# Joint 512-column products in four output projections and in the products for the memory's keys

## The chip, the cores and the metric

The kernel runs on one core of one Trainium2 chip. The metric is the device time of one execution in microseconds (us). Three runs of the kernel before gave 1250.81, 1250.83 and 1251.04 us; their median is 1250.83 us.

## The reference

Two transformer blocks follow each other on an activation of 256 tokens by 1024 features, all in float32. The first has a gated feed-forward, a mixer (latent attention with 8 heads beside differential attention with 4), an output projection, a second feed-forward and a gated embedding. The second has two layers of mixer, cross attention to a memory of 256 tokens, and feed-forward, each closed by a residual and a layer norm. Cut to what the change touches:

```python
h = h + jnp.concatenate([o_mla, o_diff], axis=-1) @ w_out[i]            # block one
h = h + 0.5 * swiglu(rms_norm(h, g_ffn2[i]), ...)
...
y = hybrid_ab_mixer(...)                 # layer 0; ends with y @ w_out; layer 1: a pooling mixer
x = layer_norm(ALPHA * x + y, ln_mix_g[l], ln_mix_b[l])
k = (mem_n @ w_k).reshape(B, -1, XA_HEADS, XA_DH)                       # keys of the memory
...
x = layer_norm(ALPHA * x + o @ w_o, ln_xa_g[l], ln_xa_b[l])
y = swiglu_ffn(x, ffn_wg[l], ffn_wu[l], ffn_wd[l])
```

## The kernel before

**Tiles and split operands.** Activations lie transposed, eight blocks of 128 features by 256 tokens. A float32 product is made of three products in the fp32r type: each weight is split into a rounded part `hi` and the rest `lo`, each activation into 256 columns of its rounded part and, beside them in the same tile, 256 columns of its rest. A weight tile of 128 by 128 then needs hi by rounded, hi by rest and lo by rounded. All three go into one PSUM accumulator of 256 columns, so that a tile takes three matmuls of 256 columns.

**The joint form**, which the kernel already has in the feed-forward products (argument `joint` of `gen_T`, line 364), lets hi pass over all 512 columns in one matmul and fills a whole PSUM bank of 512 columns. Rounded and rest come out in two halves of the bank, and they are added when the bank is read: `summed` (line 430) copies the right half to SBUF on ScalarE and adds the left half on VectorE.

```python
s = self.St(name)
self.ac.copy(s, o[:, T:])
self.ve.tensor_tensor(s, s, o[:, :T], ALU.add)
```

**Order of the work.** No scheduler reorders anything: each engine runs its instructions in the order in which the program issues them (`manual_schedule`, line 2172). A unit is eight weight tiles (1024 columns). `Net.get` (line 232), called before the products of unit u, issues the ScalarE cast that makes `hi` of unit u + 4 and the VectorE subtraction that makes `lo` of unit u + 3 (lines 319 and 343), then a step of the work put off by `later`. The weights come by DMA on the SP queue into three raw buffers.

**The output projections.** `row_tiles(NB, NB, head)` (line 739) orders the 64 tiles: the first `head` output blocks j run side by side over all eight k, so that they end together, one tile after the other; then each further block takes one unit of its own. The head is 4 for `wout` of block one (lines 902 to 910, read out by `evac_out`), 3 for `abo` of the hybrid mixer (line 1931) and 4 for `xo0` and `xo1` of the cross attentions (line 1873). Each of them reads a finished accumulator with one VectorE instruction that also adds the residual (line 904, or line 1918 in `residual`). What follows is `enter` (line 785) or `Norm.add` (line 678). Both issue, per block, on ScalarE the scaled rounded copy (line 791 or 687) and the square (line 535); on VectorE, put off by one block, the rest of the split (line 795 or 691) and the running sums (lines 547 and 550), one sum for `enter` and two for `Norm.add`.

```python
ac.activation(xs[:, :T], z, AF.Copy, scale=g)
sq = self.stats.square(z)

def rest():
    ve.scalar_tensor_tensor(xs[:, W:W + T], z, g, xs[:, :T].bitcast(F32), ALU.mult, ALU.subtract)
    self.stats.accumulate(z, sq)
```

Once the eighth block is in, `Rows` (line 623) makes the statistics between the first units of the next product: `columns` transposes the running sums on TensorE into `tot` (line 564), VectorE reduces them (line 566), GpSimd takes the reciprocal root (lines 612 and 613), and two units later TensorE broadcasts the result into `pb` (line 512). The next product needs the split blocks `xs` as its moving operand, and its own read-outs need `pb`.

**The memory's keys.** `mem_kv` (line 1488) makes eight blocks of keys for each of the two layers, one unit of products each, in a three-matmul loop of its own, read out by one ScalarE copy (line 1504). The 16 units are fillers: the program drops them (`filler.fill`) between steps of the mixers where TensorE would otherwise wait. Seven of them stand in the mixer of block one: two among its first products, three between the steps of the differential attention (`diff_s` with line 1008, `diff_c` with lines 1022 to 1281, `pt`), two between the heads of the latent attention (`mla_s`, line 1001).

Of the kernel before, what the change touches and what calls it, by code (L numbers as in the profile page):

```python
# [13 lines left out]
ALU = mybir.AluOpType  # L14
# [3 lines left out]
T = 256  # L18
D = 1024
NB = D // P  # L20
# [10 lines left out]
HEAD = 4  # L31
# [699 lines left out]
def w2(inp, name, l=0):  # L731
    return inp[name][l]


def cut(w, k, j):
    return w[k * P:(k + 1) * P, j * P:(j + 1) * P]


def row_tiles(nj, K, head=0, korder=None):

    ko = list(korder or range(K))
    t = [(j, k) for k in ko for j in range(head)]
    return t + [(j, k) for j in range(head, nj) for k in ko]
# [19 lines left out]
def first_block(n, filler):  # L763
# [136 lines left out]
    x3 = {}  # L900

    def evac_out(j, o):
        h = n.St("h")
        ve.tensor_tensor(h, H[j], o, ALU.add)
        H[j] = h
        x3[j] = enter(j, h, stat3, "g_ffn2")

    def out(yo):
        return n.gen_T("wout", row_tiles(NB, NB, O_HEAD, [4, 5, 6, 7, 0, 1, 2, 3]),
                       lambda inp, j, k: cut(w2(inp, "w_out"), k, j), yo, evac_out)  # L910

    rest = mixer(n, xm, stat2, filler, out)
    lb = lower_bound(n)
# [574 lines left out]
def mem_kv(n, l, mx):  # L1488

    KT, V = {}, {}  # L1490

    def run():
        n.packers["xk%d" % l] = lambda inp, u: np.concatenate(
            [cut(w2(inp, "xa_wk_2", l), k, u) for k in range(NB)], axis=1)
        for j in range(NB):
            o = n.ps("kT")[:, :T]
            hi, lo = n.get("xk%d" % l, j, 1024)
            for k in range(NB):
                c = slice(k * P, (k + 1) * P)
                n.mm(o, hi[:, c], mx[k][:, :T], start=(k == 0), stop=False)  # L1500
                n.mm(o, hi[:, c], mx[k][:, T:], start=False, stop=False)
                n.mm(o, lo[:, c], mx[k][:, :T], start=False, stop=(k == NB - 1))
            s = KT[j] = n.St("KT")
            n.ac.copy(s, o)
            yield
        for half in range(2):
            nm = "xv%d%d" % (l, half)
            n.packers[nm] = lambda inp, u, half=half: np.concatenate(
                [w2(inp, "xa_wv_2", l)[k * P:(k + 1) * P, half * 512:(half + 1) * 512]
                 for k in (2 * u, 2 * u + 1)], axis=1)  # L1510
            acc = [n.ps("vB"), n.ps("vB")]
            for u in range(4):
                hi, lo = n.get(nm, u, 1024)
                for i in range(2):
                    k = 2 * u + i
                    c = slice(512 * i, 512 * i + 512)
                    for t in range(2):
                        xh = mx[k][:, t * P:(t + 1) * P]
                        xl = mx[k][:, T + t * P:T + (t + 1) * P]
                        n.mm(acc[t], xh, hi[:, c], start=(k == 0), stop=False)  # L1520
                        n.mm(acc[t], xl, hi[:, c], start=False, stop=False)
                        n.mm(acc[t], xh, lo[:, c], start=False, stop=(k == NB - 1))
                if u == 3:
                    for t in range(2):
                        v = V[half, t] = n.Tt("V")
                        n.ac.copy(v, acc[t])
                yield

    return KT, V, run()


# [292 lines left out]
def cross(n, l, ln, KT, V, evac_o):  # L1824

    ac, ve, po, pe = n.ac, n.ve, n.po, n.pe
    qT = {}

    def evac_q(j, o):
        t, c = ln.apply(o, "qT", ve.tensor_copy)  # L1830
        n.later(lambda: ac.activation(t, t, AF.Identity, bias=c))
        qT[j] = t

    gq = n.gen_T("xq%d" % l, row_tiles(NB, NB, Q_HEAD), lambda inp, j, k: cut(w2(inp, "xa_wq_2", l), k, j),
                 ln.xs, ln.rows.after(evac_q), Norm.W)
    st, yo = {}, {}

    def sc(h):
        S = n.ps("S")
        for t in range(2):  # L1840
            for b in range(2):
                n.mm(S[:, t * T:(t + 1) * T], qT[2 * h + b][:, t * P:(t + 1) * P], KT[2 * h + b],
                     start=(b == 0), stop=(b == 1))
        st["E", h] = softmax_parts(n, S, scale=1.0 / 16)

    def pd(h):

        E, sm = st["E", h]
        r = n.st("rc", 2)
        po.tensor_tensor(r, sm, n.mone, ALU.pow)  # L1850
        for t in range(2):
            c = slice(t * T, (t + 1) * T)
            ac.activation(E[:, c], E[:, c], AF.Copy, scale=r[:, t:t + 1])

    def pt(h):
        o = transposed(n, st.pop(("E", h))[0])
        s = st["P", h] = n.Tt("PT")
        ac.copy(s, o)

    def pv(h):  # L1860
        s = st.pop(("P", h))
        for d in range(2):
            o = n.ps("pv")
            c = (2 * h + d) % 4 * P
            for kb in range(2):
                n.mm(o[:, :T], V[h // 2, kb][:, c:c + P], s[:, kb * T:(kb + 1) * T],
                     start=(kb == 0), stop=(kb == 1))
            yo[2 * h + d] = n.split(o[:, :T], name="yo")

    def wo_src(inp, j, k):  # L1870
        return cut(w2(inp, "xa_wo_2", l), k, j)

    go = n.gen_T("xo%d" % l, row_tiles(NB, NB, HEAD), wo_src, yo, evac_o)
    take = lambda g, c: [next(g, None) for _ in range(c)]
    n.nc.scalar.preload_act_table_set("exp_and_others")
    n.bg.append(ln.values())
    take(gq, X_Q[0])
    sc(0)
    take(gq, X_Q[1])
    pd(0)  # L1880
    sc(1)
    pt(0)
    take(gq, X_Q[2])
    pd(1)
    sc(2)
    pt(1)
    take(gq, NB)
    n.settle()
    pv(0)
    pd(2)  # L1890
    sc(3)
    n.nc.scalar.preload_act_table_set("silu_and_others")
    pt(2)
    pv(1)
    take(go, 1)
    pd(3)
    pv(2)
    pt(3)
    take(go, 1)
    pv(3)  # L1900
    take(go, 1)
    n.flush_bg()
    take(go, 10)


def second_block(n, H, xs, KT, V, filler, lb):
# [18 lines left out]
    for l in range(2):  # L1925

        ln = Norm(n, "ln_mix", l * NB, D_MIX[l], ALPHA if l else 1.0)
        if l == 0:
            yo, late = hybrid(n, X, xs, filler, lb)
            late()  # L1930
            n.stream_T("abo", row_tiles(NB, NB, A_HEAD), lambda inp, j, k: cut(w2(inp, "ab_w_out_2"), k, j),
                       yo, residual(X, ln.add))
        else:
            sc = n.st("psc", 8)
            po.tensor_scalar(sc, n.vec("pool_scale_2", 0, NB), 1.0 / ALPHA, None, ALU.mult)
            pool_mixer(n, X, xs, residual(X, ln.add, sc), filler)
        filler.through(l)
        nx = Norm(n, "ln_xa", l * NB, D_XA)
        cross(n, l, ln, KT[l], V[l], residual(ln.keep, nx.add))
        X = ln.keep  # L1940
        n.debug("mix%d" % l, [X[k] for k in range(NB)])
        ln = nx
        hd, held = {}, {}

        def evac(j, o):
            t, c = ln.apply(o, "s", ac.copy)
            if j % 2 == 0:
                act = once(lambda: ac.activation(t, t, AF.Silu, bias=c))
                n.later(act)
                held[j // 2] = t, act  # L1950
            else:
                s, act = held.pop(j // 2)
                act()
                ve.scalar_tensor_tensor(s, t, c, s, ALU.add, ALU.mult)  # L1954
                hd[j // 2] = n.split_later(s, name="hd")

        n.bg.append(ln.values(3))
        n.stream_T("g%d" % l, row_tiles(2 * NF, NB, G_HEAD),
                   lambda inp, j, k, l=l: cut(w2(inp, ("ffn_wg_2", "ffn_wu_2")[j % 2], l), k, j // 2),
                   ln.xs, ln.rows.after(evac), Norm.W)  # L1960
        n.settle()
        n.flush_bg()
        X = ln.keep
        n.debug("xa%d" % l, [X[k] for k in range(NB)])
        if l == 1:
            last_down(n, hd, X)
            break
        st = n.stats(NB, LN_EPS, True)
        n.stream_T("d%d" % l, row_tiles(NB, NF), lambda inp, j, k, l=l: cut(w2(inp, "ffn_wd_2", l), k, j),
                   hd, residual(X, lambda j, z: st.add(z), joint=range(NB - 1)), joint=range(NB - 1))  # L1970
        keep = {}
        for k in range(NB):
            keep[k] = n.St("xp", 272)
            po.memset(keep[k][:, 0:16], 0.0)
        lz = Lazy(n, st, "ln_ffn_g_2", "ln_ffn_b_2", 0,
                  keep={k: keep[k][:, 16:272] for k in range(NB)})
        lz.start(lambda: filler.fill(1), lambda: filler.fill(F_POOL[0]))
        xs = (lz, keep)
        X = lz.keep
# [212 lines left out]
```

## Time and profile before

| | |
|---|---|
| median of three runs | 1250.83 us |
| the profiled execution | 1250.96 us |
| its span, first to last instruction | 1249.2 us |
| around the span (1250.96 - 1249.2) | 1.8 us |
| TensorE busy | 1234.6 us, 99% of the span |
| VectorE busy | 985.6 us, 79% |
| ScalarE busy | 736.6 us, 59% |
| GpSimd busy | 107.5 us, 9% |
| weight DMA, 16 engines | 47.6% of their time |
| chain that ended last | 92% of it TensorE |

The table is to be read from below. The chain that ended last is the sequence of waits that set the end; nearly all of it is products. TensorE's busy time says the same, but it counts modelled ends of pipelined matmuls, so that the pace of products is better read from the number of matmuls in a stretch. VectorE's share is an average: in the output projections and behind them it is well above 79%.

### The profile page before, as it was taken

The numbers are of one execution on the slowest core, as the hardware profiler recorded it, in microseconds if no ns is written. First come the engines' busy times: TensorE is split into PE (matmuls) and PEld (weight loads), VectorE is DVE, ScalarE is ACT, GpSimd is POOL, SyncE is SP. The second block draws the span as 40 slices with busy tenths as digits, with TensorE's granted clock in tenths as the row PEclk, the third lists the DMA queues.
The fourth block names the chain that finished last, engine by engine and source line by source line (L and its number), as shares of the span: only waits on it lengthen the run. The fifth ranks groups of instructions, "written<-read, shape, count | busy, mean of one in ns | idle before, by whom it ended". The sixth has DMA issues, their size and how long they took to land.

```text
span 1249.2 us, 21526 instructions
## 1 busy us (share of the span) xinstructions
PE 1234.6 (99%) x8450; PEld 1139.2 (91%) x8450; DVE 985.6 (79%) x1821; ACT 736.6 (59%) x1363; POOL 107.5 (9%) x234
## 2 busy tenths in 40 slices
PE   8999999999999999999999999999999999999997
PEld 8988888889988898998889999999889989999985
DVE  6788966875887777689989778998668879899844
ACT  5666646676666664465466675665445676565541
POOL 1000103500000000000012120000003031000000
PEclk9999999999999999999999999999999999999999
DMA  8655556432455555544344434555555425555550
GB/s 301 226 177 193 187 186 223 152 136 68 169 189 182 202 174 199 202 169 150 121 169 152 152 105 165 203 198 175 203 178 182 161 97 184 178 203 193 188 193 34
DMA packets 32181, 216.06 MB, mean 173 GB/s; under 512 B 3728, under 2 KB 3984, under 8 KB 7376
## 3 DMA queue, kind: packets, MB, share of 16 engines
q1 hardware_dynamic: 30528, 210.62, 47.6%
q0 software_dynamic: 1120, 3.41, 0.8%
q8 instruction: 67, 1.10, 0.4%
q10 hardware_dynamic: 432, 0.66, 0.2%
q14 instruction: 34, 0.28, 0.1%
HBM read 213.62 MB, written 1.05 MB: 172 GB/s over the span
## 4 chain that ended last, share of the span: by engine, by line
PE 92%; DVE 4%; ACT 2%; DMA 1%; issue 1%; POOL 0%; DVEq 0%; SPq 0%; ACTq 0%; POOLq 0%
PE acc L354 70%; PE accB L354 6%; PE accL L354 5%; PE vB L354 4%; PE kT L354 3%; DMA raw<-wts 1%; PE S L354 1%; DVE lo L343 1%; PE pv L354 1%; PE oM L354 1%; ACT E L1015 1%; PE pt L1031 1%; PE O L354 1%; DVE sb L1008 0%; PE ds L354 0%
## 5 line engine op out<-in xcount | busy, mean ns | idle before, releaser
L354 PE MATMUL acc<-xs,hi 128*128 128x258 f32 (+2 forms) x2816 | 606.5, 306 | 1.6 <-ACT hi L319 1.6
L343 DVE TENSOR_TENSOR lo<-raw,hi 128x1024 fp32r<-128x1024 f32 (+2 forms) x395 | 472.8, 1210 | 29.3 <-ACT hi L319 29.3
L354 PEld LDWEIGHTS acc<-xs,hi 128*128 128x128 f32 x2816 | 453.4, 189 | 26.9 <-ACT hi L319 1.8
L354 PE MATMUL acc<-xs,lo 128*128 128x256 f32 (+1 forms) x1696 | 476.6, 281 | 0.5 <-DVE lo L343 0.4
L319 ACT CAST hi<-raw 128x1024 fp32r<-128x1024 f32 (+2 forms) x395 | 404.3, 1041 | 37.6 <-DMA raw<-wts 16.6
L354 PEld LDWEIGHTS acc<-xs,lo 128*128 128x128 f32 x1696 | 321.4, 190 | 0.9 <-DVE lo L343 0.9
L354 PE MATMUL acc<-hd,hi 128*128 128x512 f32 (+1 forms) x594 | 185.5, 369 | 0.0
L354 PE MATMUL acc<-hd,lo 128*128 128x256 f32 x528 | 147.9, 280 | 0.0
L354 PEld LDWEIGHTS acc<-hd,hi 128*128 128x128 f32 x594 | 107.0, 188 | 20.3
L354 PEld LDWEIGHTS acc<-hd,lo 128*128 128x128 f32 x528 | 99.4, 188 | 0.0
L354 PE MATMUL acc<-yo,hi 128*128 128x256 f32 x512 | 92.9, 284 | 0.3 <-ACT yo L467 0.2
L354 PEld LDWEIGHTS acc<-yo,hi 128*128 128x128 f32 x512 | 78.7, 188 | 1.0 <-ACT yo L467 0.5
L354 PE MATMUL acc<-yo,lo 128*128 128x256 f32 x256 | 71.8, 280 | 0.0
L460 ACT CAST hd<-s 128x256 fp32r<-128x256 f32 x88 | 35.8, 407 | 55.6 <-DVE s L1954 47.0
L354 PE MATMUL accB<-hi,xs 128*128 128x512 f32 (+1 forms) x192 | 59.7, 392 | 0.0
L354 PE MATMUL accL<-hi,hd 128*128 128x512 f32 x176 | 55.6, 397 | 0.0
L708 DVE TENSOR_TENSOR s<-acc,rows 128x256 f32<-128x256 f32 x88 | 37.0, 420 | 17.8 <-ACT c L707 17.8
L1620 DVE SCALAR_TENSOR_TENSOR cv<-up,vt,cv 128x256 f32<-128x256 f32 x120 | 50.2, 485 | 0.0
L354 PEld LDWEIGHTS acc<-yo,lo 128*128 128x128 f32 x256 | 48.3, 189 | 0.0
L354 PE MATMUL kT<-xs,hi 128*128 128x256 f32 x256 | 46.8, 284 | 0.2 <-ACT E L1015 0.2
L709 DVE SCALAR_TENSOR_TENSOR s<-rows,c,s 128x256 f32<-128x256 f32 x88 | 42.7, 485 | 3.1
L461 DVE TENSOR_TENSOR hd<-s,hd 128x256 fp32r<-128x256 f32 x88 | 37.3, 424 | 5.4 <-ACT hd L460 4.3
(330 smaller groups left out, 1563.5 us busy)
## 6 DMA issues: line engine op xcount, KB each, us to landing
raw<-wts SPq DMA_DIRECT2D x193, 1024.0 KB, 4.9
raw<-wts SPq DMA_DIRECT2D x6, 512.0 KB, 7.4
raw<-wts SPq DMA_DIRECT2D x2, 832.0 KB, 4.8
mem<-memT POOLq DMA_DIRECT2D x8, 128.0 KB, 3.6
bias<-bias POOLq DMA_DIRECT2D x4, 256.0 KB, 5.6
gb<-rows POOLq DMA_DIRECT2D x4, 256.0 KB, 6.8
x<-xT SPq DMA_DIRECT2D x3, 256.0 KB, 7.8
raw<-wts SPq DMA_DIRECT2D x1, 768.0 KB, 4.7
```

Of the source, the lines that this page charges most:

```text
L319: self.ac.copy(hi[:, c], raw[:, c])
L343: self.ve.tensor_tensor(lo[:, c], raw[:, c], hi[:, c].bitcast(F32), ALU.subtract)
L354: self.pe.matmul(out, a, b, start=start, stop=stop, **k)
L460: self.later(lambda: self.ac.copy(hi, src), lambda: self.ve.tensor_tensor(xs[:, T:], src, hi.bitcast(F32), ALU.subtract))
L461: lambda: self.ve.tensor_tensor(xs[:, T:], src, hi.bitcast(F32), ALU.subtract))
L708: ve.tensor_tensor(t, o[:, :T], R, ALU.mult)
L709: ve.scalar_tensor_tensor(t, NM, c[:, 0:1], t, ALU.mult, ALU.add)
L1015: ac.activation(E[:, c], src[:, c], AF.Exp, bias=mx[:, t:t + 1], scale=scale, accum_out=sm[:, t:t + 1] if sums is None else sums[t])
L1031: n.pe.transpose(o[:, kb * T + t * P:kb * T + (t + 1) * P], E[:, t * T + kb * P:t * T + (kb + 1) * P], n.ident)
L1620: ve.scalar_tensor_tensor(a, u[:, k:k + T], w, a, ALU.mult, ALU.add)
```

## The change

The four output projections take `joint=range(NB - 1)`: blocks 0 to 6 use the joint form and are read out by `summed` with one more VectorE instruction for the residual; block 7 stays as it was. The loop for the memory's keys becomes joint for all eight blocks, and the ScalarE copy that read it out becomes `summed`. Loads, casts, heads, and the places of the fillers are as before.

```diff
--- before.py
+++ after.py
@@ -900,14 +900,19 @@
     x3 = {}
 
     def evac_out(j, o):
-        h = n.St("h")
-        ve.tensor_tensor(h, H[j], o, ALU.add)
+        if j < NB - 1:
+            h = n.summed(o, "h")
+            ve.tensor_tensor(h, H[j], h, ALU.add)
+        else:
+            h = n.St("h")
+            ve.tensor_tensor(h, H[j], o, ALU.add)
         H[j] = h
         x3[j] = enter(j, h, stat3, "g_ffn2")
 
     def out(yo):
         return n.gen_T("wout", row_tiles(NB, NB, O_HEAD, [4, 5, 6, 7, 0, 1, 2, 3]),
-                       lambda inp, j, k: cut(w2(inp, "w_out"), k, j), yo, evac_out)
+                       lambda inp, j, k: cut(w2(inp, "w_out"), k, j), yo, evac_out,
+                       joint=range(NB - 1))
 
     rest = mixer(n, xm, stat2, filler, out)
     lb = lower_bound(n)
@@ -1493,15 +1498,14 @@
         n.packers["xk%d" % l] = lambda inp, u: np.concatenate(
             [cut(w2(inp, "xa_wk_2", l), k, u) for k in range(NB)], axis=1)
         for j in range(NB):
-            o = n.ps("kT")[:, :T]
+            o = n.ps("kT")
             hi, lo = n.get("xk%d" % l, j, 1024)
             for k in range(NB):
                 c = slice(k * P, (k + 1) * P)
-                n.mm(o, hi[:, c], mx[k][:, :T], start=(k == 0), stop=False)
-                n.mm(o, hi[:, c], mx[k][:, T:], start=False, stop=False)
-                n.mm(o, lo[:, c], mx[k][:, :T], start=False, stop=(k == NB - 1))
-            s = KT[j] = n.St("KT")
-            n.ac.copy(s, o)
+                last = k == NB - 1
+                n.mm(o, hi[:, c], mx[k][:, :2 * T], start=(k == 0), stop=last, skip_group_check=True)
+                n.mm(o[:, :T], lo[:, c], mx[k][:, :T], start=False, stop=last, skip_group_check=True)
+            KT[j] = n.summed(o, "KT")
             yield
         for half in range(2):
             nm = "xv%d%d" % (l, half)
@@ -1870,7 +1874,8 @@
     def wo_src(inp, j, k):
         return cut(w2(inp, "xa_wo_2", l), k, j)
 
-    go = n.gen_T("xo%d" % l, row_tiles(NB, NB, HEAD), wo_src, yo, evac_o)
+    go = n.gen_T("xo%d" % l, row_tiles(NB, NB, HEAD), wo_src, yo, evac_o,
+                 joint=range(NB - 1))
     take = lambda g, c: [next(g, None) for _ in range(c)]
     n.nc.scalar.preload_act_table_set("exp_and_others")
     n.bg.append(ln.values())
@@ -1929,14 +1934,14 @@
             yo, late = hybrid(n, X, xs, filler, lb)
             late()
             n.stream_T("abo", row_tiles(NB, NB, A_HEAD), lambda inp, j, k: cut(w2(inp, "ab_w_out_2"), k, j),
-                       yo, residual(X, ln.add))
+                       yo, residual(X, ln.add, joint=range(NB - 1)), joint=range(NB - 1))
         else:
             sc = n.st("psc", 8)
             po.tensor_scalar(sc, n.vec("pool_scale_2", 0, NB), 1.0 / ALPHA, None, ALU.mult)
             pool_mixer(n, X, xs, residual(X, ln.add, sc), filler)
         filler.through(l)
         nx = Norm(n, "ln_xa", l * NB, D_XA)
-        cross(n, l, ln, KT[l], V[l], residual(ln.keep, nx.add))
+        cross(n, l, ln, KT[l], V[l], residual(ln.keep, nx.add, joint=range(NB - 1)))
         X = ln.keep
         n.debug("mix%d" % l, [X[k] for k in range(NB)])
         ln = nx
```

## Rows read from the trace of the kernel before

**Rows 1.** The page, part 1: busy time, share of the span, instructions of each engine.

```profile
PE 1234.6 (99%) x8450; PEld 1139.2 (91%) x8450; DVE 985.6 (79%) x1821; ACT 736.6 (59%) x1363; POOL 107.5 (9%) x234
```

**Rows 2.** Stretch table: from:to, length, busy us per engine, granted clock, DMA share, GB/s.

```profile
375.00:400.00 25.00, 25.00 (x146) 21.92 (x145) 19.52 (x32) 15.52 (x28) 0.00 (x0) 1.00 0.54 182
```

**Rows 3.** The chain that ended last: start us, length us, work.

```profile
329.77 0.22 PE tot L564 x2
...
697.43 0.45 PE pb L512 x4
...
754.90 0.44 PE tot L564 x4
...
761.11 0.44 PE pb L512 x4
...
941.91 5.69 PE kT L354 x48
```

**Rows 4.** Groups of instructions by form, TensorE.

```profile
L354 PE MATMUL acc<-yo,lo 128*128 128x256 f32 x256 | 71.8, 280 | 0.0
...
L354 PE MATMUL kT<-xs,lo 128*128 128x256 f32 x128 | 35.9, 280 | 0.0
```

**Rows 5.** Timeline, a joint accumulator read out in the second down product.

```profile
463.72 0.37 ACT L433 COPY h<-acc 128x256 f32<-128x256 f32 x1 [1.49 <-PE acc L354]
...
464.12 0.42 DVE L434 TENSOR_TENSOR h<-h,acc 128x256 f32<-128x256 f32 x1 [0.33 <-ACT h L433]
...
464.58 0.42 DVE L840 TENSOR_TENSOR h<-h,rb 128x256 f32<-128x256 f32 x1
```

**Rows 6.** Timeline of ScalarE, two joint read-outs following each other.

```profile
336.37 0.38 ACT L433 COPY s<-acc 128x256 f32<-128x256 f32 x1
...
338.02 0.35 ACT L433 COPY u<-acc 128x256 f32<-128x256 f32 x1
```

**Rows 7.** Timeline of VectorE in several stretches.

```profile
270.28 0.16 DVE L1022 RECIPROCAL rc<-sm 128x2 f32<-128x2 f32 x1
...
281.52 0.69 DVE L1001 TENSOR_REDUCE mx<-S 128x2 f32<-128x512 f32 x1 [0.24 <-PE S L354]
...
672.53 0.74 DVE L1918 SCALAR_TENSOR_TENSOR z<-h,acc 128x256 f32<-128x256 f32 x2
...
742.81 0.41 DVE L1918 SCALAR_TENSOR_TENSOR z<-x,acc 128x256 f32<-128x256 f32 x1
...
745.34 0.41 DVE L1918 SCALAR_TENSOR_TENSOR z<-x,acc 128x256 f32<-128x256 f32 x1
...
752.54 0.41 DVE L550 TENSOR_TENSOR acc<-acc,z 128x256 f32<-128x256 f32 x1
```

**Rows 8.** Timeline of ScalarE in several stretches.

```profile
270.54 0.36 ACT L1504 COPY KT<-kT 128x256 f32<-128x256 f32 x1
...
282.74 0.38 ACT L1504 COPY KT<-kT 128x256 f32<-128x256 f32 x1
...
316.09 0.51 ACT L791 ACTIVATE xs<-h,vt 128x256 fp32r<-128x256 f32 x1
...
737.93 0.51 ACT L687 ACTIVATE xs<-z,vt 128x256 fp32r<-128x256 f32 x1
...
743.25 0.51 ACT L687 ACTIVATE xs<-z,vt 128x256 fp32r<-128x256 f32 x1 [0.77 <-DVE z L1918]
...
743.67 0.40 ACT L535 ACTIVATE sq<-z 128x256 f32<-128x256 f32 x1
...
743.98 1.04 ACT L319 CAST hi<-raw 128x1024 fp32r<-128x1024 f32 x1
...
751.58 2.94 ACT L319 CAST hi<-raw 128x1024 fp32r<-128x1024 f32 x3
```

**Rows 9.** Timeline of GpSimd, the reciprocal root of the first cross attention.

```profile
759.54 0.54 POOL L613 TENSOR_TENSOR r<-r 128x2 f32<-128x2 f32 x1
```

**Rows 10.** Stretch table, columns as in Rows 2, after the last product.

```profile
1241.30:1249.20 7.90, 0.00 (x0) 0.00 (x0) 4.38 (x13) 0.72 (x2) 0.93 (x1) 0.65 0.34 122
```

## The prediction

> **What bounds the kernel now.** I read the page's busy line first: TensorE is busy 99% of the span, VectorE 79%, ScalarE 59% [rows 1]. That says that products set the end, and it hides where VectorE has nothing left. So the second view is the chain that ended last, read only at the stages that the change touches [rows 3]. In each of the four output projections the chain passes from products through `tot` and `pb`, the two places where TensorE needs statistics that VectorE and ScalarE have summed. The third view is the timelines of VectorE and ScalarE in these stages [rows 7, 8], to see how late those two engines already are. In the first cross attention the last running sum starts at 752.54 and ends at 752.95, and TensorE asks for it at 754.90: about 2 us of slack. The reciprocal root ends at 760.08 [rows 9], `pb` starts at 761.11: 1 us of slack. This slack is what the change has to live on.
>
> **What the products gain.** 256 lo products stand in the four projections, 64 in each, and 128 in the two sets of keys [rows 4]. Seven of eight blocks become joint, so 224 tiles, and all 128 for the keys: 352 tiles go from three matmuls to two. Sixteen tiles in the old form take 5.69 us, 0.356 each [rows 3]; in a joint stretch 145 to 146 matmuls fill 25 us, one of them across the edge, which is 0.345 for a pair [rows 2]. The columns are the same 768 in both, 0.320 us at 2.4 GHz, so that what goes is the fixed cost of one matmul, about 11 ns: 352 x 0.011 = 3.8 us. The Trainium skill (TensorE: Matmul & The Clock Gate, Part 1, "Wait — 56ns, not 53.3ns?") gives about 2.5 ns for that fixed cost, by which the gain would be 0.9 us as an estimate; the rows of this kernel have four times that, and the rows decide.
>
> **What the read-out costs.** Before, one VectorE instruction per block reads the accumulator, and ScalarE then takes its two (scaled copy, square). After, ScalarE has to copy first. Its queue is in order, so that the copy of block j+1 stands behind the square of block j, the square behind the residual sum of block j on VectorE, and that behind the copy of block j. Two queues that ran apart become one ring. The links, start to start: copy to sum 0.40 and sum to a dependent instruction 0.46 [rows 5]; residual sum to scaled copy 743.25 - 742.81 = 0.44 [rows 7, 8]; scaled copy to square 0.42, square to the next 0.31 [rows 8]. A head block takes 0.40 + 0.46 + 0.44 + 0.42 + 0.31 = 2.03 us. That such a ring forms here is seen where joint read-outs already follow each other: copies at 336.37 and 338.02, 1.65 us apart, with one ScalarE instruction in the ring in place of two [rows 6]. A later block has the cast of a coming unit in the ring as well, (2.94 - 1.04) / 2 = 0.95 [rows 8], which makes 2.98; and VectorE's own cycle, 745.34 - 742.81 = 2.53 before, plus the dependent 0.46, makes 2.99 [rows 7]. One unit of joint products takes 8 x 0.345 = 2.76. So the ring is slower than the products and falls behind block by block, after a head that alone costs it several microseconds.
>
> **First cross attention, worked out.** ScalarE gets to the head at 737.93 [rows 8]. Copies of blocks 0 to 3 start 2.03 apart, the fourth at 744.02; blocks 4, 5 and 6 follow 2.99 apart, block 6 at 752.99, its residual sum at 752.99 + 0.40 + 0.46 = 753.85. In the trace of before block 5's starts at 745.34 and, one cycle of 2.53 on, block 6's at 747.87; from there to the last running sum are 752.54 - 747.87 = 4.67 [rows 7]. The last sum now starts at 758.52, 5.97 later. TensorE would reach `tot` a little earlier than 754.90 and stands until 758.9. The reduction and the root keep their distance to that sum, so that the root ends at 760.08 + 5.97 = 766.05, where TensorE, two units after `tot`, would be ready at 765: `pb` moves from 761.11 to 766.05, **+4.95 us**. The second cross attention repeats the pattern with the same distances (one stands for two): **+4.95**.
>
> **Block one's projection.** ScalarE gets to the head at 316.09 [rows 8]. Three rings of 2.03 and three of 2.98 put the copy of block 6 at 331.12. The tail from there to the end of the last sum is 758.93 - 752.99 = 5.94 in the cross attention; here each block has one running sum, not two, which takes three times 0.41 at most off [rows 7], so 4.7 to 5.0: 336.0. `tot` was at 329.77 [rows 3]: **+6.3**. Root and `pb` have two units of cover behind it.
>
> **The hybrid's projection.** The head has three blocks and four follow. VectorE starts it at 672.53 [rows 7]; two units of keys run just ahead, each with a new sum of 0.34 to 0.42 in VectorE's queue, say 673.3. Then 2 x 2.03 + 4 x 2.99 + 0.46 + 4.67 = 21.2 to the last sum, 694.45, and 760.08 - 752.54 = 7.54 to the root, 702.0. `pb` was at 697.43 [rows 3]: **+4.6**.
>
> **The keys.** Most of the 16 units stand where TensorE is the bound. In block one's mixer some don't: VectorE is in the chain there, and the new sum makes it wait for ScalarE's copy. For the third unit in the differential steps the copy ends at 270.54 + 0.36 = 270.90, where VectorE would go on at 270.28 [rows 7, 8]: 0.65 of wait and 0.34 of sum. The two units before it cost 0.7 and 0.3 in the same way, 2.0 together. In the latent attention the copy ends at 283.12, and the maximum behind it, at 281.52 before, can't start before 283.5; the next exponential, which came right behind the copy, at about 283.0, then waits for that maximum, 0.69 long, until 284.2: 1.2. The keys cost **+3.2** in that mixer; nothing at the one unit later in it. The ends of this term are 0.3 x 4 = 1.3, the sums alone, and 3.9.
>
> **The sum.** 4.95 + 4.95 + 6.3 + 4.6 + 3.2 = 24.0. Of the 3.8 gained, what lies in stages that now wait for the ring is lost; what is left are nine units of keys and seven early units of three projections, 16 x 8 x 0.011 = 1.4. That is +22.6 on the profiled execution's 1250.96 (span 1249.2 and 1.8 around it): 1273.6, and the median stands 0.13 below that execution: 1273.4. With each of the four projections 1 us up or down and the keys between their ends, this case alone spans 1268 to 1278. New PSUM use is nothing: the banks were 512 columns wide already. Casts, loads and DMA count are the same; their dates move with the rings.
>
> **The rivals.**
> *The products' gain is all there is.* If the read-outs hide, the time falls by 3.8 to 1247.0. For it speaks that VectorE and ScalarE are idle 21% and 41% [rows 1]. It decides if a ring takes under 2.76 us per block and the heads clear within the slack of 2 us; the rows say 2.99, and 8 us for a head. The Trainium skill (Perfetto Trace Analysis, "Matmuls") says that larger matmuls are more efficient; by that rule this case would be it.
> *Queues don't lock.* If the copies run ahead, and only VectorE's 0.33 per block counts, 7 x 0.33 = 2.3 us eats the slack: about +1.4 in block one, +1.2 to +1.3 at each of the other three, +1.3 for the keys, less 1.4: +5, 1256. Against it stands the ring of rows 6.
> *The clock falls too.* By the sum TensorE stands some 4 us at `tot` in three stages and longer in block one. After the last product, when TensorE has nothing to do for 7.9 us, the mean granted clock is 0.65 [rows 10], so it does fall to 1.2 GHz within such a wait. Two units follow before `pb`, 5.7 us; at 1.2 GHz all through they would take 5.7 more. Between nothing and that in four places, I take 2.5 each: +10, 1283. The Trainium skill (TensorE: Matmul & The Clock Gate, "HAM oscillation") has a kernel whose clock falls again at every wait between bursts; that is this rival.
>
> **How the numbers follow.** The ring 0.66, the clock 0.16, unlocked queues 0.10, the gain alone 0.08. A measurement of this kernel can tell about 0.2%, 2.5 us, from no change. Faster by more takes the gain alone: 0.07. Within it lie the fringes of that case and of the unlocked queues: 0.04. Slower: 0.89. The range holds the ring's own span and the clock's with its upper bound cut, and reaches down halfway to the unlocked queues: 1262 to 1286; about 0.18 is outside.
>
> **What would show it.** Right: in each projection, copies of line 433 about 2.0 us apart in the head and 3.0 after, `tot` waiting for the running sum by 4 to 5 us, `pb` in the cross attentions waiting for the root, pairs of products at 0.345 in the keys, and the line of running sums as the chief releaser of TensorE. Wrong: copies that follow each other within 1 us, `tot` without a wait, or waits that the later feed-forward wins back. A clock below 1.00 behind `tot` would show the third rival.

## The result and the profile after

The changed kernel takes **1281.22 us** (median of four runs, 1279.37 to 1281.93), the kernel before 1250.89 us beside it: a ratio of 1.0239, with a 95% interval of 1.0227 to 1.0251. The forecast was 1273.4 us, in a range of 1262 to 1286.

From the page of the changed kernel's profile, busy time and share of the span:

```profile
span 1279.7 us, 20870 instructions
...
PE 1246.3 (97%) x8098; PEld 1130.1 (88%) x8098; DVE 1003.6 (78%) x1865; ACT 744.5 (58%) x1391; POOL 107.3 (8%) x234
```

Against [rows 1] TensorE has 352 instructions fewer and is busy 12 us longer, while its share falls from 99% to 97%. So it stood more, and fewer instructions kept it busy for longer. The first is in the view of waits, TensorE alone (us in total, times, longest), after:

```profile
PE tot L564 <- DVE acc L550: 7.9, 3, 5.0
PE acc L354 <- DVE lo L343: 4.2, 5, 1.2
PE acc L354 <- DVE xs L691: 4.0, 4, 1.6
```

and before, where the third is not there:

```profile
PE acc L354 <- DVE lo L343: 0.4, 1, 0.4
PE tot L564 <- DVE acc L550: 0.3, 1, 0.3
```

All three are VectorE's: running sums, the `lo` parts of the weights and the second half of the split. They stand in the same queue as the read-outs.

How the read-outs get late is in the chain that ended last (start, length, work). Before, from the third unit of block one's projection to `tot`, it held products alone:

```profile
312.65 17.11 PE acc L354 x135
```

After, it goes round between two engines:

```profile
320.30 0.28 ACT h L433
320.58 0.02 issue
320.61 0.43 DVE h L434
321.04 0.02 issue
321.06 0.44 DVE h L905
321.50 0.02 issue
321.52 0.51 ACT xs L791
322.03 0.31 ACT sq L535
322.34 0.26 ACT h L433
```

This is one turn of the forecast's ring: copy, sum, residual sum, scaled copy, square, and then the next block's copy, 322.34 - 320.30 = 2.04 us later. The copies of the first cross attention, in ScalarE's timeline, show head and later blocks beside each other:

```profile
756.23 0.35 ACT L433 COPY z<-acc 128x256 f32<-128x256 f32 x1
758.25 0.35 ACT L433 COPY z<-acc 128x256 f32<-128x256 f32 x1
760.27 0.35 ACT L433 COPY z<-acc 128x256 f32<-128x256 f32 x1
762.30 0.35 ACT L433 COPY z<-acc 128x256 f32<-128x256 f32 x1
765.25 0.36 ACT L433 COPY z<-acc 128x256 f32<-128x256 f32 x1
768.24 0.36 ACT L433 COPY z<-acc 128x256 f32<-128x256 f32 x1
771.24 0.36 ACT L433 COPY z<-acc 128x256 f32<-128x256 f32 x1
```

2.02 and 2.03 in the head; 2.95, 2.99 and 3.00 from there. A single turn in the four projections is off these values: 2.66 at the start of the hybrid's head, where VectorE was still at two `lo` parts.

That TensorE also ran slower is in the stretch table (columns as in [rows 2]; the granted clock is the third number from the end). These four stretches, one for each projection, are all there are before the last product:

```profile
339.30:346.10 6.80, 5.71 (x19) 4.97 (x20) 5.99 (x9) 3.22 (x6) 1.61 (x1) 0.50 0.81 275
707.90:711.30 3.40, 3.40 (x17) 3.40 (x17) 3.40 (x4) 3.40 (x4) 0.00 (x0) 0.50 0.37 106
776.20:779.60 3.40, 3.40 (x18) 3.26 (x17) 3.40 (x6) 3.40 (x4) 0.00 (x0) 0.51 0.12 22
1083.40:1086.80 3.40, 3.40 (x18) 3.40 (x18) 3.40 (x6) 3.40 (x5) 0.00 (x0) 0.51 0.04 14
```

0.50 is 1.2 GHz. What TensorE did ahead of each is in its timeline (the wait, in brackets, ends where the instruction starts):

```profile
340.39 0.66 PE L564 MATMUL tot<-ct,acc 128*128 128x128 f32 x2 [4.99 <-DVE acc L550]
...
707.76 0.99 PE L564 MATMUL tot<-ct,acc 128*128 128x128 f32 x4 [2.64 <-DVE acc L550]
...
773.07 0.35 PE L354 MATMUL acc<-xs,hi 128*128 128x258 f32 x1 [0.42 <-DVE xs L691]
...
775.61 0.36 PE L354 MATMUL acc<-xs,hi 128*128 128x258 f32 x1 [1.58 <-DVE xs L691]
```

In block one and in the hybrid it stood at `tot`. In the cross attentions it stood a little earlier, in the feed-forward's head, for the split of the last blocks; by the time it came to `tot`, the sums were there.

The second cross attention repeats the waits of 0.42 and 1.58 (1080.60 and 1083.13).

Set beside the kernel before, the views give the time by stage. `tot` of block one starts at 340.39; before, in the same view, at 329.61 ([rows 3] have it at 329.77, where the chain takes it up):

```profile
329.61 0.38 PE L564 MATMUL tot<-ct,acc 128*128 128x128 f32 x2
```

Of these 10.8 us, 4.4 come from the keys ahead of the projection, as the run of the keys alone shows below, so the projection has 6.4. `pb` behind it starts 13.4 later than before: 2.6 more on the way between the two, and 5.7 us of that way lie in the first half-speed stretch. From there to the end of the hybrid mixer 0.7 are won back (+12.7 at 668.02). The hybrid's projection adds 5.6 (`pb` 697.43 to 715.70), the first cross attention 5.7 (761.11 to 785.07), the pooling layer 0.4, the second cross attention 5.5 (24.36 late at the values' products of 980.92, 29.84 at `pb` of 1092.45). The last 0.8 comes behind that, in a feed-forward that was not touched.

### The profile page after: what moved, and what is told of

It is laid out like the page before. It is cut to its first block, busy times and chain, and to the rows that moved or that the text cites. A ratio compares the mean times of both kernels' runs of the same rounds, so it can differ in the third digit from the quotient of the medians.

```text
span 1279.7 us, 20870 instructions
## 1 busy us (share of the span) xinstructions
PE 1246.3 (97%) x8098; PEld 1130.1 (88%) x8098; DVE 1003.6 (78%) x1865; ACT 744.5 (58%) x1391; POOL 107.3 (8%) x234
## 4 chain that ended last, share of the span: by engine, by line
PE 81%; DVE 11%; ACT 5%; issue 1%; DMA 1%; POOL 0%; DVEq 0%; SPq 0%; ACTq 0%; POOLq 0%
PE acc L354 62%; PE accL L354 5%; PE accB L354 4%; PE vB L354 3%; DVE lo L343 3%; PE kT L354 2%; ACT E L1020 1%; DMA raw<-wts 1%; DVE acc L550 1%; ACT hi L319 1%; PE S L354 1%; DVE z L1918 1%; DVE z L434 1%; PE pv L354 1%; DVE xs L691 1%
## 5 line engine op out<-in xcount | busy, mean ns | idle before, releaser
L354 PE MATMUL acc<-xs,hi 128*128 128x258 f32 (+2 forms) x2816 | 614.4, 308 | 5.5 <-DVE xs L691 4.0
L354 PEld LDWEIGHTS acc<-xs,hi 128*128 128x128 f32 x2816 | 458.4, 190 | 31.9 <-issue 4.7
L354 PE MATMUL acc<-yo,hi 128*128 128x512 f32 (+1 forms) x288 | 92.3, 375 | 0.7 <-DVE yo L468 0.7
L354 PEld LDWEIGHTS acc<-yo,hi 128*128 128x128 f32 x288 | 51.9, 188 | 11.1 <-DVE yo L468 0.9
L354 PE MATMUL kT<-xs,hi 128*128 128x512 f32 x128 | 46.1, 400 | 0.2 <-ACT E L1020 0.2
```

The source lines that it names most:

```text
L354: self.pe.matmul(out, a, b, start=start, stop=stop, **k)
```

## The experiments

All ran beside the kernel before on their chip, which took 1250.9 to 1251.1 us there. Three theories were open: the ring, the clock, and a mere load of more instructions on VectorE and ScalarE. The first two runs split the change in its two parts, with the two after them inside each.

**Only the keys.** The loop of `mem_kv` as changed, the four projections as before.

> The kernel before, with the joint loop for the memory's keys alone. Waiting theory (VectorE's new sum waits for ScalarE's copy in the mixer of block one): the third unit of the block-one projection starts about 4.2 us later, as it did in the changed kernel (312.65 to 316.81), and nine units elsewhere gain 0.04 each: +3.9, 1254.8. Rival, only the sums' own time on VectorE counts: 4 x 0.34 less 0.35, +1.0, 1251.9.

1256.16 us, ratio 1.0045 (1.003 to 1.006): **+5.1**, 1.2 over the value with the waits. `tot` of block one comes at 334.20, 4.4 late. VectorE's timeline shows where the last part of it arises, at the key between two heads of the latent attention:

```profile
285.64 0.42 DVE L434 TENSOR_TENSOR KT<-KT,kT 128x256 f32<-128x256 f32 x1 [1.88 <-ACT KT L433]
285.98 0.68 DVE L1001 TENSOR_REDUCE mx<-S 128x2 f32<-128x512 f32 x1
286.57 1.28 DVE L1318 TENSOR_TENSOR dn<-oD,ss 128x512 f32<-128x512 f32 x2
```

VectorE stands 1.88 us for ScalarE's copy, which itself stands behind a cast of 1.04 us. The maximum was at 281.52 [rows 7] and is 4.46 later; the maximum of the head before it, at 278.14 and before at 275.67, was 2.47 late. So this one key costs 2.0, and what lies ahead, the differential attention with its three keys above all, 2.5.

**The keys, with the sum put off.** ScalarE's copy is issued at once, VectorE's sum behind the next step's instructions:

```diff
-            KT[j] = n.summed(o, "KT")
+            s = KT[j] = n.St("KT")
+            n.ac.copy(s, o[:, T:])
+            n.later(lambda s=s, o=o: n.ve.tensor_tensor(s, s, o[:, :T], ALU.add))
```

> As the keys alone, but the VectorE sum is put off to the next unit of weights, so that it no longer stands right behind ScalarE's copy. Waiting theory: the waits go and the sums stay, about +1.0, 1251.9. Rival, the sum itself is the cost wherever it stands: as the keys alone, +3.9, 1254.8.

1253.13 us, ratio 1.0016 (1.0007 to 1.0026): **+2.1**. That is between the two expected values. Taking the sum away from its place behind the copy gives back 3 of the 5 us. The 2.1 that stay go by the forecast's reading to the sum itself, in a queue that is in the chain; no run shows it by itself. It is no gain even so.

**Only the projections.** The other half: joint projections, keys as before.

> The changed kernel with the old loop for the keys: the four projections alone. If the two parts add up: 1281.2 less the keys' 3.9 and 0.8 at the head of the hybrid's projection, 1276.5. If the keys' delay was hidden behind the projections' waits: 1281.

1274.96 us, ratio 1.0189 (1.0172 to 1.0206): **+23.9**. With the keys alone 29.0, against 30.3 for the whole change: the parts add within the spread of the runs (1273.89 to 1276.79 here). The clock stands at half in the same four places.

**Plain heads.** As the run before, but only the three or four blocks between a head and the last are joint:

```diff
-        if j < NB - 1:
+        if O_HEAD <= j < NB - 1:
             h = n.summed(o, "h")
...
-                       joint=range(NB - 1))
+                       joint=range(O_HEAD, NB - 1))
```

> The four projections alone, joint only for the blocks behind the head (three, four, three and three of them). Ring theory: no ring in the head, 0.46 more per later block, so that the running sums end 1.3 to 1.9 us later than before against a slack of 1 to 2 us: about +0.5 in each cross attention, +0.8 in the hybrid's, +1.3 in block one's, +3.3 in all, 1254, and no half-speed clock behind the statistics. If each joint block cost the same wherever it stands: 13 of 28 blocks, +12, 1263.

1254.19 us, ratio 1.0027 (1.0016 to 1.0038): **+3.1**. Joint heads cost 20.8 of the 23.9, the slower clock behind them included. TensorE waits 1.8 us at `tot` in all, 1.5 the longest, and the clock stays at 2.4 GHz up to the last product.

**Only the projection of block one**, so that one stage stands alone:

> The kernel before with block one's projection alone in the joint form. Ring theory: the statistics' transposes come 6.5 us later (as in the changed kernel), and the clock falls to 1.2 GHz in that wait, so that two units behind it take 7.9 us and not 5.6, and a little more: +6.5 + 2.8 = +9.3, 1260.2. Ring without clock: +6.5, 1257.4.

1259.35 us, ratio 1.0067 (1.005 to 1.0084): **+8.3**. The wait at `tot` is 4.98, as in the changed kernel, and the clock falls, but in the profiled execution for 3.4 us and not for 6.8. The length seems to vary from one execution to the next: two of the four have a mean clock of 0.997 and take 1258.87 and 1259.02 us, two have 0.995 and take 1259.68 and 1260.09.

**The same with TensorE kept at work.** Nineteen products of constants stand ahead of `tot`, where TensorE would wait. They compute nothing that is used:

```diff
     def columns(self):
+        if self.busy and not self.net.dry:
+            o = self.net.ps("busy")
+            for i in range(self.busy):
+                self.net.mm(o[:, :P], self.net.ones, self.net.ones, start=(i == 0), stop=(i + 1 == self.busy))
         self.r = self.stats.rms() if self.scales else self.stats.norm_cols()
```

> As block one's projection alone, with 19 products of a constant into an unused PSUM bank ahead of the statistics' transposes, about 4 us of TensorE work in a wait of 5; they change nothing that is computed. Clock theory: the granted clock stays at 1.00 and the 2.8 us behind the wait go: +6.5, 1257.4. If the clock costs nothing, or if the products delay the transposes: 1260 or more.

1257.48 us, ratio 1.005 (1.0035 to 1.0065). The stretch from `tot` to `pb`, without the constant products (first) and with them (second, another kernel):

```profile
336.00:343.30 7.30, 7.29 (x34) 6.41 (x35) 4.91 (x6) 3.14 (x4) 1.61 (x1) 0.78 0.85 310
```

```profile
335.90:342.00 6.10, 5.93 (x35) 5.27 (x36) 5.07 (x7) 3.31 (x4) 1.61 (x1) 1.00 0.83 301
```

`tot` comes at the same time (336.01 and 336.07), the clock stays at 2.4 GHz, and the time is 1.9 us less. So in this run **the clock costs 1.9 us** (1.3 to 2.7 by the single executions) **and the late sums 6.5**. In the changed kernel, with 6.8 us at half, it costs more in this stage: the 2.6 us between `tot` and `pb`.

**No copy on ScalarE.** The joint projections alone, but VectorE adds both halves itself, one behind the other:

```diff
-            h = n.summed(o, "h")
-            ve.tensor_tensor(h, H[j], h, ALU.add)
+            h = n.St("h")
+            ve.tensor_tensor(h, H[j], o[:, :T], ALU.add)
+            ve.tensor_tensor(h, h, o[:, T:], ALU.add)
```

> The four projections alone in the joint form, read out without ScalarE: VectorE adds the residual to the left half, then the right half, which is as many VectorE instructions as in the changed kernel. Ring theory: VectorE's own 0.46 per block is left, seven blocks, 3.2 us later against the slack: about +2.2 in each cross attention, +2.1 in the hybrid's, +1.9 in block one's, less 0.5: +7.9, 1258.8. Rival, VectorE's load is the cause and the order of the queues isn't: as with the copy, about 1276.5.

1260.12 us, ratio 1.0071 (1.0056 to 1.0086). VectorE has the same number of instructions per block as in the run of the projections alone, and 14.8 us are gone. The clock is a part of that: it fell here in block one alone, for 3.4 us behind a stand of 1.94 us at `tot`. But the clock is worth about 5 us in all four stages, as the last run shows, so about 10 are left, an estimate: a load on VectorE is not what costs them.

**Copies of a head first.** The same instructions as in the projections alone, in another order:

```diff
+    def copies_first(self, j, o, take, name, head):
+        s = self.St(name)
+        if j < NB - 1:
+            self.ac.copy(s, o[:, T:])
+        if j < head - 1:
+            self.waiting = getattr(self, "waiting", []) + [lambda: take(s, o)]
+            return
+        for f in getattr(self, "waiting", []):
+            f()
+        self.waiting = []
+        take(s, o)
```

> The four joint projections as before (1274.96 alone), with the same instructions in another order: the copies of a head's blocks (four, three in the hybrid's) are issued to ScalarE one behind the other, ahead of the first block's sum. If the order of the two queues makes the ring, the head goes at VectorE's own pace, as where VectorE read both halves itself (1260.1), plus one copy of 0.35 to 0.4 per stage: 1260 to 1263, with the copies of a head about 0.3 us apart. If the copies' and sums' load makes it late, whatever the order, it stays at about 1275.

1264.85 us, ratio 1.0108 (1.0093 to 1.0123): 10.1 us less than in the changed order, 2 us over the expected band. ScalarE's timeline of the first cross attention, where four copies go in one piece:

```profile
745.34 1.18 ACT L440 COPY z<-acc 128x256 f32<-128x256 f32 x4
...
752.15 0.36 ACT L440 COPY z<-acc 128x256 f32<-128x256 f32 x1
755.14 0.36 ACT L440 COPY z<-acc 128x256 f32<-128x256 f32 x1
```

From the first copy to the fifth it now takes 6.81 us; in the changed kernel 765.25 - 756.23 = 9.02. Nothing but the order in ScalarE's queue differs, so the head's ring is an effect of order. From the fifth block on the distance is 2.99, as it was. In the cross attentions the run without a ScalarE copy goes no faster there (VectorE alone needs 2.98 per block), but in block one its blocks follow each other in 2.65, and these in 2.97: that is part of why this order stays behind it. The clock still falls in block one (TensorE stands 3.7 us at `tot`), and stays at 1.00 in the other three stages. Part of the 10.1 is therefore clock and not order. How much was not separated; by the about 5 us that the clock is worth in all four stages (below), an estimate, at least half of it is order.

**The whole change with TensorE kept at work.** Constant products in all four stages, to price the clock.

> The whole change, and products of constants, whose results nobody reads, where TensorE stood in it: 19 ahead of the totals in block one (it stood 4.99 us there), 11 ahead of those after the hybrid (2.64), and 2 and 7 ahead of the two products on late tiles in the feed-forward behind each cross attention (0.42 and 1.58); one of them took 4.40 / 19 = 0.23 us in the run of block one's projection alone. In the changed kernel the granted clock was at half for 6.8, 3.4, 3.4 and 3.4 us in these four stages, 17.0 us in all. If the clock fell because TensorE stood, and that is what the forecast's sum left out, the clock stays at 1.00 to the last product and the time falls by up to 17.0 / 2 = 8.5 us, from 1281.2 to about 1273. If the excess over the sum is late statistics and not the clock, the products gain nothing: 1280 to 1283.

1277.34 us, ratio 1.0207 (1.019 to 1.0224). The clock stays at 1.00 to the last product, but only 3.9 come back, not 8.5. The timeline of TensorE in the first cross attention says what was wrong with the experiment itself (a constant product counts as two matmuls there):

```profile
770.47 0.61 PE L354 MATMUL busy<-ones 128*128 128x128 f32 x4
770.84 0.36 PE L354 MATMUL acc<-xs,hi 128*128 128x258 f32 x1
772.34 0.36 PE L354 MATMUL acc<-xs,hi 128*128 128x258 f32 x1 [1.14 <-DVE xs L702]
...
773.01 1.72 PE L354 MATMUL busy<-ones 128*128 128x128 f32 x14
774.49 0.48 PE L354 MATMUL acc<-xs,hi 128*128 128x258 f32 x2
```

The seven constant products stand behind the wait that they should have filled, and delay the next tile. They were moved one tile forward:

> As the run before it with constant products, with those in the two feed-forwards one tile earlier. There TensorE still stood 0.39 and 1.14 us for the sixth and seventh late tile of the cross attention, and the constant products came only behind that, so that the totals were reached 1.2 and 0.7 us later than the stage before them would give (1.5 us of constant products, less what the clock gave back). Two now stand ahead of the sixth tile and seven ahead of the seventh. If that was all, TensorE no longer stands there beyond 0.3 us, the clock stays at 1.00, and each of the two stages gives back about 1.5 us: 1274.3. If the stretch behind those tiles is set by other late work (casts on VectorE), it stays at 1276 to 1278.

1276.15 us, ratio 1.02 (1.0183 to 1.0217). That is 1.2 us less by the medians, where 3.0 were expected, and in the band of the second alternative; between the two profiled executions, 1278.61 and 1275.77, it is 2.8, and each kernel's four runs spread over 1.7 to 2.0, so the two alternatives are not told apart. TensorE no longer stands for the split blocks, and the clock is 1.00 in all four stages:

```profile
340.00:347.00 7.00, 6.40 (x38) 5.70 (x39) 5.50 (x8) 3.88 (x5) 1.61 (x1) 1.00 0.81 297
705.00:713.00 8.00, 7.55 (x60) 6.95 (x60) 7.32 (x12) 4.96 (x6) 2.17 (x2) 1.00 0.67 249
774.00:782.00 8.00, 7.76 (x65) 7.30 (x64) 7.12 (x11) 3.90 (x5) 2.17 (x2) 1.00 0.68 245
1079.00:1088.00 9.00, 8.76 (x70) 8.33 (x70) 7.61 (x13) 4.78 (x7) 3.46 (x5) 1.00 0.66 242
```

The clock is thus worth about **5 us** of the 30 (the runs of both kernels spread over 1.7 to 2.6). That is less than half of the 17.0 us spent at half speed. TensorE stood through 1.1 of these (339.30 to 340.39), and in the three later stages the reciprocal root comes next: from `tot` to `pb` the changed kernel takes 7.78, 7.01 and 6.85 us, this one 6.48, 6.41 and 6.41, and TensorE now waits 0.19 us at `pb` for GpSimd's result, as in the line below, where the changed kernel had no wait:

```profile
781.36 0.43 PE L520 MATMUL pb<-ct,r 128*128 128x128 f32 x2 [0.19 <-POOL r L621]
```

None of these kernels beats the one before.

## Why the prediction was right, and where it fell short

**The direction and its mechanism were right.** But for one turn of 2.66, the ring takes 2.02 to 2.08 us per head block, and 2.95 to 3.00 after, where the forecast had 2.03 and 2.98 to 2.99, link by link. That it is what costs the time is shown by three runs that each break it in another way: plain heads (+3.1 in place of +23.9), no copy on ScalarE (+9.1) and another order in the queue (+13.8). Each of them frees more than the 5 us or so that the clock is worth. The rival with unlocked queues falls with the same rows, and so does the one in which the products' gain is all there is. The Trainium skill's rule behind that rival (Perfetto Trace Analysis, "Matmuls", larger matmuls are more efficient) holds in this trace for the products by themselves, and decides nothing about the kernel.

**The projections' terms** were near: block one +6.4 up to `tot` for a forecast of 6.3; the hybrid +5.6 for 4.6, the cross attentions +5.7 and +5.5 for 4.95 each, and these three have the clock in them. In the last run, where the clock stays up, they are 4.3, 5.2 and 4.5. What TensorE waits for was wrong in three places. The forecast let it stand at `tot` in the cross attentions, and it stood for `xs`, two microseconds ahead of it. It stood 0.5 to 1.2 us in each projection for a `lo` part, which the forecast did not have. And it had `pb` of the cross attentions wait for the root: in the changed kernel TensorE, at half speed, came later than the root, and the wait, of 0.19 us, appears where the clock stays up there.

**The step that failed is the clock**, which stood as a rival and not in the sum. The forecast had TensorE stand 4 us in three stages and longer in one, and knew a fall within 7.9 us from [rows 10], yet gave the clock 0.16. It fell in all four stages. The rival had 2.5 us each, 10 in all; the runs show about 5 for the four, of which 2.6 are in block one. So the size was twice what came, and the chance far too small. The rule cited beside that rival (the Trainium skill, TensorE: Matmul & The Clock Gate, "HAM oscillation"), a fall at every wait between bursts, agrees with these four stretches at 0.50 and 0.51. It does not hold for every wait here: in the kernel with plain heads, whose longest wait at `tot` is 1.5 us, there is no fall, and with the copies of a head first none behind the waits of 1.58 and 1.59 us in the cross attentions.

**The keys were mis-sized**: +3.2 was the term, and 4.4 arise in that mixer. The differential part came to 2.5 for 2.0. In the latent attention the sum and the wait delay the maximum from 281.52 by 2.0, as the forecast had it ("can't start before 283.5"). From there the forecast followed the next exponential, 1.2 late. But the step behind the maximum in VectorE's own queue is in the chain as well (line 1318, and TensorE's transposes wait 0.8 for it), and all of the 2.0 went through.

**The products' gain was mis-sized too**, without much weight: 0.345 per tile had come from counting matmuls in 25 us, where one more at either edge counts; by its starts the same stretch has 0.348 (71 pairs from 375.00 to 399.72). In the stretch of keys that TensorE bounds, 24 tiles are one row of the chain, before (first) and after (second):

```profile
948.04 8.52 PE kT L354 x72
```

```profile
972.52 8.40 PE kT L354 x48
```

0.350 per tile against 0.355: 5 ns each, half of the forecast's 11. On all 352 tiles that is 1.8 us, and by these rows the whole change had no more than this to win.

With the clock (5) added to the sum of 22.6, the keys 1.2 to 1.9 larger and the kept gain 0.7 smaller, the terms come to 1280 to 1281. The forecast was right in sign and cause, and 8 us short. That 1281.2 lies inside its range is owed to the rival of the clock: the ring's own span ended at 1278.

**What stays open.** The last 0.8 us of the changed kernel, in the feed-forward behind the second cross attention, is one row of the chain, before (first) and after (second):

```profile
1063.05 114.96 PE acc L354 x960
```

```profile
1092.89 115.75 PE acc L354 x960
```

The same 960 products follow each other without a stand, each 0.8 ns slower. So no wait is behind it. The run of the keys alone has the slower pace (115.75); the one with the sum put off and the one with the keys as before (114.96 both) do not. Why the pace differs was not found. It is 2.5 ns per tile of three products, half of the 5 ns that were read above as the gain of a joint tile, so that gain is no firmer than this.

## What to carry to other kernels

Before a product is made cheaper at the price of a longer read-out, write down the read-out's chain across both engines and close it: if block j+1's first instruction stands behind block j's last on an in-order queue, the period is the sum of the links (here 2.0 us, against a head's accumulator finished every 0.35), however idle the engines look on the page. It bites where several accumulators end together and statistics of all of them are needed next; such heads should keep the one-instruction read-out, or have their copies issued ahead of everything else. And a forecast that makes TensorE stand for several microseconds should price the slower clock behind that wait in its sum.

## What the runs showed of the hardware

The clock was at 1.2 GHz for 6.8 us in block one, where TensorE had stood 4.99 us, and for 3.4 us after waits of 2.64 us or of 0.42 and 1.58 with work between. These are shorter stands than the 7.9 us at the end of the kernel before [rows 10], behind which alone it had fallen there. With VectorE reading both halves it fell for 3.4 us behind a stand of 1.94, and with the copies of a head first it did not fall behind stands of 1.58 and 1.59. The same stand of 4.98 us was followed by 3.4 us at half speed in one profiled execution and, at 4.99, by 6.8 in another. So in these runs the length of the last stand alone says neither whether the clock falls nor for how long.

Products of constants, 4.40 us of them, kept the clock up where they filled a wait, and `tot` came no more than 0.06 us later (336.07 after 336.01). Where they stood behind the wait that they should have filled they kept it up as well, but held up the next tile. And of the 17.0 us at half speed only about 5 came back.
